# New ranks, gate counts and matmul estimates for the planner of a woven instruction order

## The chip, the core and the metric

The kernel runs on one core of one Trainium2 chip. A core has five engines that run side by side, each with its own fixed order of instructions: TensorE (PE in the profile; its weight loads stand apart as PEld), VectorE (DVE), ScalarE (ACT), GpSimd (POOL) and SyncE (SP), which issues most DMA transfers. Engines wait for each other by semaphores. The metric is the time of one execution on the device in microseconds, as the median of several runs.

## The reference

One layer of a diffusion backbone, batch 1, 256 latent tokens and 256 context tokens, width 2048, all in fp32. Cut to what matters:

```python
h  = modulate(rmsnorm(x, norm1_w), sh1, sc1)       # latent tokens
hc = modulate(rmsnorm(ctx, norm1_w), csh1, csc1)   # context tokens
cols = h @ w_in                                    # and hc @ w_in: one combined projection
# branch a, RWKV-7: 16 heads of 64, in both directions, context first
s = s * w_t - (s @ kk_t) * b_t + v_t * k_t ; y_t = s @ r_t
# branch b, gated DeltaNet: 8 heads of 128, chunks of 64, in both directions
sol = triangular_solve(lmat, rhs)                  # unit lower triangular, per chunk
s = s * gl_i + kt_i.T @ (u_i - w_i @ s)
# merge, output projection, SwiGLU with 5632 hidden columns
m = sigmoid(g_a) * (o_a @ p_a) + sigmoid(g_b) * (o_b @ p_b)
x = x + gt1 * (m @ w_out)
x = x + gt2 * swiglu(modulate(rmsnorm(x, norm2_w), sh2, sc2), w_gate_up, w_down)
return rmsnorm(x, final_norm_w)
```

## The kernel before

A large matmul of this kernel (a gemm below) splits each fp32 operand into a high and a low part in a faster format and adds three products: high by high, high by low, low by high. The weights are loaded as raw fp32 (tile `wraw`), ScalarE casts the high part (`whi`) and VectorE subtracts to get the low part (`wlo`). One gemm of the projection has 16 slices of the contraction, so 48 matmuls, with 512 columns (k and v, latent and context) or 256 (r, q and the gates, latent alone).

The kernel has a first part (modulation, norm, the low-rank columns), the woven part, and then merge, output projection and feed-forward, written straight. Only the woven part is planned. It holds 8 pairs of RWKV heads, then 8 DeltaNet heads, and 86 projection gemms. Each piece of the work is a Python generator that yields its next operation, a list of operations, or the name of something it waits for:

- per pair `p`: `prepare` (token shift, decays, keys), `grams` for each direction (products of 64x64 tiles), `inverse` (triangular inverses by 16x16 blocks, with a trip through DRAM scratch, then 32x32 tiles on PE in PSUM tile `pi`), `values`, `scan` (eight dependent steps with 64-row tiles in PSUM tile `s`);
- per DeltaNet head `h`: `features` (convolution, norm), `tokens` (transposes), `decays`, `head_grams`, `head_inverse`, `head_scan`; `begin` runs once before them;
- `lowrank` and 32 `lowrank_out` for the low-rank decays and rates that every pair needs;
- `products`, which runs the gemms one after the other, with `cast` for their weights (two gemms ahead at most) and `gate_out` to store a gate;
- `ada_rest` with its `row_tile`s, modulation rows on VectorE.

The planner `Weave` keeps a clock for each engine ("lane"). In each turn `Weave.run` takes the piece whose next operation can start earliest, and among those that could start at the same time the one with the lowest rank. It emits the operation and adds its estimated cost, and for PE a charge `turn` when the shape of tile changes. The order in which operations were emitted is the order in which each engine runs them on the chip; the estimates themselves have no part in the execution. `hop` is the assumed delay from one engine to another, `own` that on the same engine, `dma` that of a transfer. `products` has the highest rank number among the users of PE, so gemm matmuls go in wherever nothing else can start.

The costs stand in `Lane` (lines 126 to 137), the constants `LAT` and `GATES_A`, `GATES_B` at lines 28 to 30, the ranks in the calls of `weave.add`. All woven operations are recorded under line 145 in the profile, since one helper issues them; tiles tell them apart. Gemm matmuls write `mm`.

Forty of the 86 gemms are gates, which nothing in the weave waits for. `products` takes the first gemm of its list whose need is met, and the gates stand last in the list. `GATES_A[p]` gates may be taken once pair `p - 1` is prepared, `GATES_B[h]` once the Gram products of head `h` are done:

```python
todo += [("g", p, ("prepared", p - 1, 0) if p else None) for p in range(NPAIR) for _ in range(GATES_A[p])]
todo += [("g", h, ("gram", h)) for h in range(NGH) for _ in range(GATES_B[h])]
```

Head `h + 2` reuses buffers of head `h`: `tokens`, `decays` and `head_grams` of `h + 2` wait for the scan of `h`. Each inverse waits for the one before it.

Of the kernel before, what the change touches and what calls it, by code (L numbers as in the profile page):

```python
# [18 lines left out]
P = 128  # L19
D = 2048  # L20
KT = D // P
T = 256
# [2 lines left out]
NPAIR = 8  # L25
NGH = 8
DECAY = 0.6065306597126334
GATES_A, GATES_B = ((6, 3, 0, 2, 3, 3, 1, 3), (3, 0, 0, 0, 0, 2, 6, 8))

LAT = dict(dma=2.4, hop=0.3, own=0.1, grp=32, crank=-1, cg=4, turn=0.13)  # L30
LNEXP = "natural_log_exp_and_others"
SIGM = "sigmoid_and_others"
UNIT = 64 * 64 + 64
# [77 lines left out]
class Lane:  # L111
# [5 lines left out]
    def __getattr__(self, name):  # L117

        def op(out, *a, **k):
            if name == "preload_act_table_set":  # L120
                return Op(self, 1.3, lambda: self.engine.preload_act_table_set(out))
            if name == "dma_start":
                return Op(self, 0.6 if self.each > 0.002 else 0.06, lambda: self.engine.dma_start(out, *a))
            n = int(np.prod(out.shape[1:]))
            kind = "full"
            if name == "transpose" and len(a) == 2:
                cost = 0.109
            elif name == "matmul":
                rows, m = a[0].shape[0], out.shape[0]
                if a[0].dtype == F32R:  # L130
                    cost, kind = 0.0035 + 0.000448 * n, "split"
                elif rows <= 64 and m <= 64:
                    cost, kind = 0.026 if rows < 64 else max(0.06, 0.05 + 0.00015 * n), (rows, m)
                elif m <= 64:
                    cost, kind = 0.085 if m == 64 else 0.12, (rows, m)
                else:
                    cost = (0.0054 + 0.00167 * n) * (1.22 if rows == 96 else 1)
            else:
                psum = a and getattr(a[0], "tensor", None) is not None and "PSum" in type(a[0].tensor).__name__
                cost = (self.psum if psum else self.fixed) + self.each * n  # L140
# [4 lines left out]
            return Op(self, cost, lambda: getattr(self.engine, name)(out, *a, **k), kind)  # L145
        return op


class Loads:
# [121 lines left out]
def emit(ctx: ExitStack, tc, A, out, dbg=None):  # L271
# [4 lines left out]
    weave = Weave()  # L276
# [132 lines left out]
    with tc.tile_pool(name="p0", bufs=1) as p0, \  # L409
# [31 lines left out]
        ps = pst(pa, "pa")  # L441
# [276 lines left out]
    def lowrank():  # L718
# [17 lines left out]
        for p in range(NPAIR):  # L736
# [8 lines left out]
            for j in (0, 2, 1, 3):  # L745
                ps = yield psb
                yield e.matmul(ps, w[:96, 4 * (p % 2) + j], lin[:, j], start=True, stop=True)
                weave.add(2, lowrank_out(p, j, ps, out[j]))

    def prepare(p):  # L750

# [75 lines left out]
        yield v.scalar_tensor_tensor(kb, kb, p_("rk", p), r, ALU.mult, ALU.mult)  # L827
        weave.ready("keys", p)
        if p + 1 < NPAIR:
            weave.add(10 * p + 13, prepare(p + 1))  # L830

    def grams(p, d):
        o = pr[p]
# [3 lines left out]
        def m4(a, b, rows):  # L837
# [1 line left out]


        p1, p2 = yield pab, pab
        yield [e.matmul(ps[h if src is ic else half[1 - j], 64 * c:64 * c + 64], src[h, T + 64 * c:T + 64 * c + 64],
                             lc[h, c, j, :], start=True, stop=True)
                    for c in range(4) for ps, src in ((p1, ic), (p2, kt)) for j, h in enumerate(half)]
        yield v.tensor_mul(LT[:, d, 4:8, :], c3(p1[:, 0:T]), m4(0, 64, slice(0, P)))
        weave.release(pab)
        for j in range(2):
# [4 lines left out]
        yield [e.matmul(ps[h if src is ic else half[1 - j], P * c:P * c + P], src[h, 64 * c:64 * c + 64], la[h, c, j, :],  # L852
                             start=True, stop=True) for c in range(4) for ps, src in ((p1, ic), (p2, kt)) for j, h in enumerate(half)]
# [183 lines left out]
    def products():  # L1037
# [24 lines left out]
        while todo or nxt:  # L1062
            if nxt is None:
# [3 lines left out]
                    continue  # L1067
                if nxt[0] == "g":
                    nxt = "g", next(gate_next)
                weave.add(LAT['crank'], cast(source(*nxt), i))  # L1070
            what, p = nxt
            nxt = choose()
            if nxt is not None:
                if nxt[0] == "g":
                    nxt = "g", next(gate_next)
                weave.add(LAT['crank'], cast(source(*nxt), i + 1))
            ps = yield mmb
            n = 512 if what in "kvKV" else T
            for k in range(KT):
# [6 lines left out]
                    weave.ready("read", i, k // 8)  # L1086
            i += 1
            if what == "g":
                weave.add(150, gate_out(rs, p, ps))
            else:  # L1090
                (hd if what in "KVQ" else pr)[p][what + "ps"] = ps
                weave.ready(what + "gemm", p)
# [326 lines left out]
    def ada_rest():  # L1419
# [23 lines left out]
        for i in range(4 * KT):  # L1443
            if i > 2:
                yield "added", i - 3
            if i % 8 == 0 and i:
                yield "gscan", i // 8 - 1
            weave.add(500, row_tile(i))
            if i % KT == KT - 1:
                b = i // KT  # L1450
                yield "added", i
# [288 lines left out]
```

## Time and profile before

| what | us |
|---|---|
| median of 3 runs | 2293.3 |
| lowest, highest | 2292.33, 2308.79 |
| span of the profiled execution, first to last instruction | 2286.3 |
| median less that span | 7.0 |
| PE busy in the span | 2184.5 |
| DVE, ACT busy in the span | 1561.3, 1056.6 |

The profile gives the execution that it records by its span; the time of a run holds some microseconds more around it. A busy time is the union of the instructions of an engine. Matmuls overlap, and the end of each is modelled, so a busy PE can still be one whose matmuls do not follow each other as fast as they could: the distance between starts tells that. In a row of grouped instructions stand line, engine, operation, written and read tiles, shape, count, then busy time, mean ns of one, and the idle time just before with what ended it. PEclk is the granted clock of TensorE.

### The profile page before, as it was taken

To read this page: it belongs to the slowest core of one execution; us is meant where nothing else is said; L and a number is where in the kernel's file an instruction comes from. 1 tells how busy PE (TensorE), PEld (TensorE's weight loads), DVE (VectorE), ACT (ScalarE), POOL (GpSimd) and SP (SyncE) were. 2 spreads that over 40 slices of the span, in tenths; PEclk is the share of its full clock that TensorE was granted. 3 is DMA by queue.
4 is the path that set the end of the run, shared out by engine and by line. 5 is a ranking of instruction groups with operands and counts; after the bars stand their busy time and mean duration, and the time that the engine had idled before them with its cause. 6 is when DMAs were issued, how large, how long until landed. Compare 5 with 4: busy or idle time off the path is not lost. (4 is left out here: it accounts for less than half of the span.)

```text
span 2286.3 us, 54678 instructions
## 1 busy us (share of the span) xinstructions
PE 2184.5 (96%) x22904; PEld 1925.0 (84%) x22904; DVE 1561.3 (68%) x3225; ACT 1056.6 (46%) x1922; POOL 110.3 (5%) x185
## 2 busy tenths in 40 slices
PE   7998999999999999999999989899999999999998
PEld 4766577777777788888888889889999999999997
DVE  3446588888877586899997668774656656444444
ACT  3245554544555554444453445444444444444443
POOL 0000000000000010111110040000000000000000
PEclk9999999999999999999999989999999999999999
DMA  9955643443443254555566696864777776566665
GB/s 384 407 148 170 187 113 89 117 106 99 106 101 100 87 180 141 162 163 165 167 188 216 232 350 230 283 207 142 237 238 236 236 233 214 186 185 192 186 189 162
DMA packets 231926, 430.76 MB, mean 188 GB/s; under 512 B 114944, under 2 KB 129152, under 8 KB 227328
## 3 DMA queue, kind: packets, MB, share of 16 engines
q1 hardware_dynamic: 203744, 350.72, 49.5%
q0 software_dynamic: 14112, 51.39, 7.1%
q10 hardware_dynamic: 13824, 25.17, 3.3%
q8 instruction: 179, 2.93, 0.5%
q14 instruction: 67, 0.55, 0.1%
HBM read 401.44 MB, written 25.77 MB: 187 GB/s over the span
## 5 line engine op out<-in xcount | busy, mean ns | idle before, releaser
L361 DVE TENSOR_TENSOR wlo<-wraw,whi 128x1024 fp32r<-128x1024 f32 x328 | 393.4, 1199 | 336.5 <-ACT whi L360 332.9
L360 ACT CAST whi<-wraw 128x1024 fp32r<-128x1024 f32 x328 | 337.5, 1029 | 469.2 <-PE mm L371 434.4
L145 PE MATMUL mm<-hxh,wlo 128*128 128x256 f32 (+1 forms) x1376 | 466.3, 339 | 7.3 <-DVE wlo L145 6.9
L145 PE MATMUL mm<-hxh,whi 128*128 128x256 f32 (+1 forms) x1376 | 464.7, 338 | 6.0 <-ACT whi L145 5.8
L145 PE MATMUL mm<-hxl,whi 128*128 128x256 f32 (+1 forms) x1376 | 462.2, 336 | 0.0
L372 PE MATMUL mm<-hfh,wlo 128*128 128x256 f32 x1344 | 374.9, 279 | 0.3 <-DVE wlo L361 0.3
L370 PE MATMUL mm<-hfh,whi 128*128 128x256 f32 x1344 | 374.9, 279 | 0.0
L371 PE MATMUL mm<-hfl,whi 128*128 128x256 f32 x1344 | 374.7, 279 | 0.0
L145 PEld LDWEIGHTS mm<-hxh,wlo 128*128 128x128 f32 x1376 | 262.4, 191 | 35.5 <-DVE wlo L145 10.0
L145 PEld LDWEIGHTS mm<-hxh,whi 128*128 128x128 f32 x1376 | 262.6, 191 | 33.3 <-ACT whi L145 7.2
L145 PEld LDWEIGHTS mm<-hxl,whi 128*128 128x128 f32 x1376 | 262.3, 191 | 25.2 <-issue 5.7
L145 DVE TENSOR_TENSOR wlo<-wraw,whi 128x512 fp32r<-128x512 f32 x344 | 236.1, 689 | 59.3 <-ACT whi L145 58.0
L372 PEld LDWEIGHTS mm<-hfh,wlo 128*128 128x128 f32 x1344 | 252.7, 188 | 0.5 <-DVE wlo L361 0.5
L370 PEld LDWEIGHTS mm<-hfh,whi 128*128 128x128 f32 x1344 | 252.8, 188 | 0.0
L371 PEld LDWEIGHTS mm<-hfl,whi 128*128 128x128 f32 x1344 | 252.7, 188 | 0.0
L145 ACT CAST whi<-wraw 128x512 fp32r<-128x512 f32 x344 | 205.0, 618 | 94.2 <-PE mm L145 56.9
L145 DVE TENSOR_TENSOR arena<-arena 128x512 f32<-128x512 f32 (+12 forms) x538 | 132.9, 248 | 28.2 <-DMA arena<-scr 13.5
L370 PE MATMUL mm<-za,whi 128*128 128x256 f32 x512 | 142.9, 279 | 0.0
L372 PE MATMUL mm<-za,wlo 128*128 128x256 f32 x512 | 142.7, 279 | 0.0
L371 PE MATMUL mm<-za,whi 128*128 128x256 f32 x512 | 142.7, 279 | 0.0
L370 PEld LDWEIGHTS mm<-za,whi 128*128 128x128 f32 x512 | 96.3, 188 | 0.0
L371 PEld LDWEIGHTS mm<-za,whi 128*128 128x128 f32 x512 | 96.3, 188 | 0.0
(318 smaller groups left out, 3907.5 us busy)
## 6 DMA issues: line engine op xcount, KB each, us to landing
wraw<-w SPq DMA_DIRECT2D x172, 512.0 KB, 4.1
wraw<-wgu SPq DMA_DIRECT2D x168, 512.0 KB, 4.5
aw<-ada_rest POOLq DMA_DIRECT2D x96, 512.0 KB, 5.2
aw<-ada_first SPq DMA_DIRECT2D x32, 1024.0 KB, 11.6
wraw<-wdn SPq DMA_DIRECT2D x64, 448.0 KB, 3.6
wraw<-wout SPq DMA_DIRECT2D x32, 512.0 KB, 4.8
aw<-ada_gt ACTq DMA_DIRECT2D x64, 256.0 KB, 4.8
wraw<-wdn SPq DMA_DIRECT2D x32, 512.0 KB, 3.6
```

The source lines that it names most:

```text
L145: return Op(self, cost, lambda: getattr(self.engine, name)(out, *a, **k), kind)
L360: S.copy(hi[:, c, :M], raw[:, c, :M])
L361: V.tensor_sub(lo[:, c, :M], raw[:, c, :M], hi[:, c, :M].bitcast(F32))
L370: E.matmul(ps, hi, Xh[:, k, :n], start=first and i == 0, stop=False)
L371: E.matmul(ps, hi, Xl[:, k, :n], start=False, stop=False)
L372: E.matmul(ps, lo, Xh[:, k, :n], start=False, stop=last and i == len(wt) - 1)
```

## The change

Three things change, all in what the planner reads; no operation is added, removed or given other operands.

The ranks, so far plain numbers at each `weave.add` (10 times the pair, 100 plus 10 times the head, plus a small number), come from a table `RANK`. The gate counts are new; their sum stays 40. Of the estimates, `hop`, `own` and `turn` are new; a matmul of 32-row tiles, of 64x64 tiles and of 128x64 tiles has a new cost; and the Gram products of the pairs, whose consecutive calls use four different 64x64 corners of the array, are charged half by a new function `quad`.

```diff
-GATES_A, GATES_B = ((6, 3, 0, 2, 3, 3, 1, 3), (3, 0, 0, 0, 0, 2, 6, 8))
-
-LAT = dict(dma=2.4, hop=0.3, own=0.1, grp=32, crank=-1, cg=4, turn=0.13)
+GATES_A, GATES_B = (10, 5, 6, 0, 1, 4, 3, 0), (0, 3, 0, 0, 0, 0, 4, 4)
+
+RANK = dict(cast=-24, lowrank=-14, prepare=24, grams=24, inverse=-1, values=7, scan=-60, begin=101, head_scan=144, head_inverse=44, head_grams=193, decays=99, tokens=163, features=141, gate_out=71, lowrank_out=42, row_tile=435)
+LAT = dict(dma=2.4, hop=0.299, own=0.072, grp=32, cg=4, turn=0.179)
...
                 elif rows <= 64 and m <= 64:
-                    cost, kind = 0.026 if rows < 64 else max(0.06, 0.05 + 0.00015 * n), (rows, m)
+                    cost, kind = (0.01 + 0.00037 * n if rows < 64 else 0.01 + 0.00075 * n), (rows, m)
                 elif m <= 64:
-                    cost, kind = 0.085 if m == 64 else 0.12, (rows, m)
+                    cost, kind = 0.058 if m == 64 else 0.14, (rows, m)
...
+def quad(ops):
+    for o in ops:
+        o.cost *= 0.5
+    return ops
...
-                weave.add(2, lowrank_out(p, j, ps, out[j]))
+                weave.add(RANK['lowrank_out'], lowrank_out(p, j, ps, out[j]))
...
-            weave.add(10 * p + 13, prepare(p + 1))
+            weave.add(10 * p + 10 + RANK['prepare'], prepare(p + 1))
...
-        yield [e.matmul(ps[h if src is ic else half[1 - j], 64 * c:64 * c + 64], src[h, T + 64 * c:T + 64 * c + 64],
+        yield quad([e.matmul(ps[h if src is ic else half[1 - j], 64 * c:64 * c + 64], src[h, T + 64 * c:T + 64 * c + 64],
                              lc[h, c, j, :], start=True, stop=True)
-                    for c in range(4) for ps, src in ((p1, ic), (p2, kt)) for j, h in enumerate(half)]
+                    for c in range(4) for ps, src in ((p1, ic), (p2, kt)) for j, h in enumerate(half)])
...
-                weave.add(LAT['crank'], cast(source(*nxt), i))
+                weave.add(RANK['cast'], cast(source(*nxt), i))
...
-                weave.add(150, gate_out(rs, p, ps))
+                weave.add(RANK['gate_out'], gate_out(rs, p, ps))
...
-            weave.add(500, row_tile(i))
+            weave.add(RANK['row_tile'], row_tile(i))
...
-        weave.add(2, lowrank())
-        weave.add(3, prepare(0))
+        weave.add(RANK['lowrank'], lowrank())
+        weave.add(RANK['prepare'], prepare(0))
         for p in range(NPAIR):
             for d in range(2):
-                weave.add(10 * p + 2, grams(p, d))
-            weave.add(10 * p + 1, inverse(p))
-            weave.add(10 * p + 4, values(p))
-            weave.add(10 * p, scan(p))
-        weave.add(100, begin())
+                weave.add(10 * p + RANK['grams'], grams(p, d))
+            weave.add(10 * p + RANK['inverse'], inverse(p))
+            weave.add(10 * p + RANK['values'], values(p))
+            weave.add(10 * p + RANK['scan'], scan(p))
+        weave.add(RANK['begin'], begin())
         for h in range(NGH):
-            for i, piece in enumerate((head_scan, head_inverse, head_grams, decays, tokens, features)):
-                weave.add(100 + 10 * h + i, piece(h))
+            for piece in (head_scan, head_inverse, head_grams, decays, tokens, features):
+                weave.add(10 * h + RANK[piece.__name__], piece(h))
```

More of the change, by code (lines that the diff above doesn't have):

```diff
@@ L851, in grams @@
         p1, p2 = yield pab, pab
-        yield [e.matmul(ps[h if src is ic else half[1 - j], P * c:P * c + P], src[h, 64 * c:64 * c + 64], la[h, c, j, :],
-                             start=True, stop=True) for c in range(4) for ps, src in ((p1, ic), (p2, kt)) for j, h in enumerate(half)]
+        yield quad([e.matmul(ps[h if src is ic else half[1 - j], P * c:P * c + P], src[h, 64 * c:64 * c + 64], la[h, c, j, :],
+                             start=True, stop=True) for c in range(4) for ps, src in ((p1, ic), (p2, kt)) for j, h in enumerate(half)])
         pv = p1.rearrange("p (c t) -> p c t", t=P)
@@ L1075, in products @@
                     nxt = "g", next(gate_next)
-                weave.add(LAT['crank'], cast(source(*nxt), i + 1))
+                weave.add(RANK['cast'], cast(source(*nxt), i + 1))
             ps = yield mmb
```

## Prediction

> **What bounds the kernel now.** I read the page first: the busy shares and the two strips over the span.
>
> ```profile
> span 2286.3 us, 54678 instructions
> ...
> PE 2184.5 (96%) x22904; PEld 1925.0 (84%) x22904; DVE 1561.3 (68%) x3225; ACT 1056.6 (46%) x1922; POOL 110.3 (5%) x185
> ...
> PE   7998999999999999999999989899999999999998
> ...
> PEclk9999999999999999999999989999999999999999
> ```
>
> TensorE (PE) carries the whole span; no other engine comes near it on average. The diff can act only between the first and the last woven instruction, so I cut the span by stage with the view of windows: start of the weave, pairs, heads, last heads, and what lies before and behind.
>
> ```profile
> core 0: us, PE busy (x) PEld busy (x) DVE busy (x) ACT busy (x) POOL busy (x), PEclk, DMA share, GB/s
> 0.00:130.00 130.00, 113.58 (x1340) 81.19 (x1341) 54.33 (x147) 37.06 (x70) 0.41 (x5) 0.97 0.97 365
> 130.00:260.00 130.00, 111.20 (x892) 78.21 (x890) 72.72 (x163) 73.93 (x123) 3.01 (x7) 0.95 0.60 181
> 260.00:820.00 560.00, 546.54 (x7843) 421.30 (x7840) 444.62 (x1108) 282.64 (x702) 19.95 (x49) 1.00 0.40 106
> 820.00:1180.00 360.00, 350.84 (x3540) 297.09 (x3539) 316.21 (x807) 172.97 (x341) 40.35 (x61) 1.00 0.57 167
> 1180.00:1312.00 132.00, 122.16 (x1399) 115.36 (x1397) 97.72 (x249) 61.14 (x130) 10.62 (x19) 0.96 0.65 209
> 1312.00:2287.00 975.00, 940.20 (x7900) 931.87 (x7900) 575.69 (x753) 428.87 (x560) 35.98 (x46) 0.98 0.68 218
> ```
>
> The weave is 1182 us. PE is idle in its four stages for 18.8, 13.5, 9.2 and 9.8 us, together 51.3. In the first and the last the granted clock is 0.95 and 0.96, which is 130 x 0.05 = 6.5 and 132 x 0.04 = 5.3 us of lost clock. Everything else is PE at work. The number of matmuls stays as it is, so a new order can only win idle time, lost clock, and what PE loses when it changes from one shape of tile to another. DVE at 316 of 360 us is the second engine among the heads.
>
> What PE waits for, within the weave (waits of PE, 130 to 1312 us):
>
> ```profile
> PE mm L145 <- DVE wlo L145: 6.9, 10, 1.8
> PE pa L145 <- ACT arena L145: 6.2, 6, 2.1
> PE pi L145 <- DVE arena L145: 6.1, 7, 2.3
> PE mm L145 <- ACT whi L145: 5.8, 5, 1.9
> PE pi L145 <- issue: 4.0, 6, 1.3
> PE s L145 <- DVE Vn L145: 3.9, 5, 2.7
> ```
>
> There is no single late resource: the gemms wait for the two casts (12.7 us), the inverses (pi) for VectorE or the sequencer (10.1 us), the others for small pieces. These are places where PE's fixed order got to an instruction earlier than the other engines' orders did.
>
> **The change part by part: the estimates.** The planner lays out every engine's order by its own costs. The rows of PE over 3 us of a pair, and two groups of Gram products, tell how good these are. An fp32 matmul stands in the trace as two records, so x64 is 32 calls and x8 is 4.
>
> ```profile
> 599.81 0.28 PE L145 MATMUL mm<-hxl,whi 128*128 128x256 f32 x1
> ...
> 601.91 0.28 PE L145 MATMUL mm<-hxl,whi 128*128 128x256 f32 x1
> 602.03 0.28 PE L145 MATMUL mm<-hxh,wlo 128*128 128x256 f32 x1
> 602.24 0.45 PE L145 MATMUL s<-VX,LAl 128*64 128x64 f32 x8
> 602.62 0.38 PE L145 MATMUL mm<-hxh,whi 128*128 128x256 f32 x1
> 602.93 0.73 PE L145 MATMUL pi<-arena 32*32 32x16 f32 x64
> 603.59 0.45 PE L145 MATMUL s<-R,Tx 64*64 64x64 f32 x8
> 603.87 0.39 PE L145 MATMUL s<-VX,C 64*64 64x128 f32 x4
> ...
> 615.71 1.24 PE L145 MATMUL pa<-LAl,arena 64*64 64x128 f32 x32
> 616.88 0.38 PE L145 MATMUL mm<-hxh,wlo 128*128 128x256 f32 x1
> ```
>
> Starts count here, not durations. Gemm to gemm is 0.117 us (19 steps from 599.81 to 602.03). Going from a gemm to a small tile takes 0.21, so 0.09 more. The lone gemm at 602.62 holds PE for 0.31, so a return and a new entry cost 0.19 together. With that, a visit of 32 calls of 32x32 tiles takes 0.66 + 0.19 = 0.85 us. The old estimate is 32 x 0.026 + 2 x 0.13 = 1.09, the new one 32 x 0.0159 + 2 x 0.179 = 0.87: now right. A visit of four 128x64 calls takes 0.38 + 0.19 = 0.57; old 4 x 0.085 + 0.26 = 0.60, new 4 x 0.058 + 0.358 = 0.59: no difference. Sixteen Gram calls with 128 columns take 1.17 + 0.19 = 1.36; old 1.37, new (halved by quad) 16 x 0.053 + 0.358 = 1.21: now too short by 0.15. So the old estimates were fair already, and the repair is mostly at the inverses, which is where PE came early and waited.
>
> ```profile
> L145 PE MATMUL pi<-arena,Tx 32*32 32x16 f32 x1536 | 17.6, 182 | 9.3 <-DVE arena L145 5.0 <-issue 4.0
> L145 PE MATMUL pi<-arena 32*32 32x16 f32 x1024 | 10.9, 180 | 0.8 <-DVE arena L145 0.8
> ```
>
> These are 24 and 16 visits of 64 records, each planned 0.22 us too long, 8.8 us in all, and 10.1 us of idle stand before them. I take 8.8, less the sixteen Gram visits that are now planned short (16 x 0.15 = 2.4): a gain of 6.4. Bounds: all 10.1 gained, or nothing gained and 2.4 lost. Behind a wait that goes, the same VectorE chain is late next, so the gain is no more than the idle shown.
>
> **The ranks.** Among the pairs the sequence of what runs side by side (scan of one, inverse and values of the next, Gram products and preparation of the one after) stays, and only its distances widen; scans 0 to 3 now go ahead of the casts. Among the heads it turns: the inverse goes first, decays ahead of the scan, Gram products last. No instruction and no wait is added; the same DMA issues, weight loads and the scratch transfers of the inverses among them, stand in another order in SP's queue. The rank of lowrank_out goes from 2 to 42, so that pair 0 passes the low-rank outputs, for all of which the preparation of pair 1 waits:
>
> ```profile
> L145 ACT ACTIVATE lo<-s,PR 128x512 f32<-128x512 f32 x32 | 21.9, 687 | 26.5 <-PE s L145 21.4 <-DMA sgd__1342<-lo 4.5 <-PE pa L145 0.5
> ```
>
> At worst pair 1 comes 22 us later; four more gates at the start (below) are 22 us of PE to hide it, and without them it would be 22 us of idle. At best the 18.8 us of idle there go. Where a cast now waits behind a scan's ScalarE copy, a gemm is late by one copy; the cover is the pair of casts made ahead. For a price below and above nothing: the gemms' cast waits are 12.7 us, and could double or go.
>
> **The gate counts.** Forty gate gemms are PE's filler. Cumulated over the pairs they were released 6, 9, 9, 11, 14, 17, 18, 21 and are now 10, 15, 21, 21, 22, 26, 29, 29. Behind the Gram products of heads 5, 6 and 7 there were 2 + 6 + 8 = 16; now 0 + 4 + 4 = 8. A gate is 48 matmuls of 0.117 = 5.6 us of PE, two 512 KB loads on SP's queue, four casts each on ScalarE and VectorE, and one copy out.
>
> ```profile
> wraw<-w SPq DMA_DIRECT2D x172, 512.0 KB, 4.1
> ...
> L145 ACT CAST whi<-wraw 128x512 fp32r<-128x512 f32 x344 | 205.0, 618 | 94.2 <-PE mm L145 56.9 <-issue 18.1 <-DMA wraw<-w 13.2
> L145 DVE TENSOR_TENSOR wlo<-wraw,whi 128x512 fp32r<-128x512 f32 x344 | 236.1, 689 | 59.3 <-ACT whi L145 58.0
> ```
>
> Per gate that is 2.5 us of ScalarE and 2.8 of VectorE. Four more at the start cost 10 and 11 us of engines that are busy 74 and 73 of 130 us there, with DMA at 0.60: they fit, and can fill PE while low-rank outputs drain. The 8 gates taken from the heads free 22 us of VectorE where it is scarce. The moved PE time itself is neither won nor lost.
>
> **The sum.** Start, pairs and first heads have 41.5 us idle and 6.5 us of lost clock. With the estimates worth 6.4, and ranks and fillers worth half of what remains, (48 - 6.4)/2 = 20.8, that is 27; I take 24, since the last heads, with fewer fillers, should rather lose 3 or 4 than gain. Half is a choice: PE already fills 97% of the pairs and heads, and a rearranged order makes waits of its own. The profiled execution has a span of 2286.3 us, the median of the three runs is 2293.3, so 7.0 lie around the span. Forecast: 2262.3 in the span, **2269 us** at the median, 1.1% less. Its own range is 2250 to 2288.
>
> On the clock: the rows have 0.95 and 0.96 where the longest single wait on PE is 2.7 us. The Trainium skill, "TensorE: Matmul & The Clock Gate", Part 1, says that PE falls to half clock after an idle window of about 3.4 us. By it none of these waits would cost clock and the sum would lack 3 us, 2272; the trace disagrees, and I go with the trace. On the tiles: the 0.09 and 0.19 us above fit what the skill says in "TensorEngine Tiling (Array Packing)", Key Properties, that a change of tiling mode drains TensorE; this speaks against ranks that jump to a small tile as soon as it is ready.
>
> **Rivals.** First, **the last heads starve** (slower). From the last PT product of head 7 to the end of the weave:
>
> ```profile
> 1225.19 0.40 DVE L145 TENSOR_TENSOR PT<-pa,arena 128x256 f32<-128x256 f32 x1
> 1226.18 0.42 DVE L145 STREAM_TRANSPOSE T<-LT 64x256 f32<-64x256 f32 x1
> ...
> 1280.51 0.62 ACT L145 COPY TF<-Tx 64x512 f32<-64x512 f32 x1
> ...
> 1310.20 0.28 PE L145 MATMUL mm<-hxh,wlo 128*128 128x256 f32 x1
> ...
> L145 ACT COPY arena<-mm 128x256 f32<-128x256 f32 x9 | 3.3, 372 | 19.9 <-PE mm L145 11.1 <-issue 8.8
> ```
>
> The inverse of head 7 starts at once and takes 54 us, its scan and the end 30 more; nine gates (50 us of PE) lie beside it. With four, 28 us of that cover are gone. If the chain keeps its 85 us, PE idles for 28 and loses about 5 of clock: 2293 + 33 = 2326, or 2302 with the gains of the forecast elsewhere. For it: the inverse begins 1 us after its input, so nothing is ahead of it to remove. Against it: much of the 54 us is queueing between gemms and row tiles, and the inverse now ranks first. It decides from the point where the chain stays over 57 us.
>
> Second, **Gram products ranked last stretch the heads** (slower). Features of the next head now go ahead of them on VectorE:
>
> ```profile
> L145 DVE SCALAR_TENSOR_TENSOR arena<-mm,PR,arena 128x508 f32<-128x508 f32 (+3 forms) x96 | 62.2, 648 | 4.5 <-ACT arena L145 4.1
> ```
>
> Twelve per head are 7.8 us. Heads h and h+2 are chained by the scan that frees the buffers, so three rounds would lose 23 us, with hardly a gate there to fill it: 2316. It needs the next head's gemms to be done by then.
>
> Third, **fewer changes of tile as well**. The new planner charges 0.179 for each, so its order may make fewer. A visit costs 0.19; the timeline of PE has seven returns from small tiles to the gemm in the 25 us from 600 (the first is that at 602.62), some 160 for the 560 us of the pairs, and as many again for the start and heads by a like rate: 60 us in all. A third of it is 20: 2249.
>
> Fourth, **nothing to tell**: new waits take the place of the old, 2286 to 2293. It includes that the estimates, fair before, hardly change the plan.
>
> **How the numbers follow.** The forecast 0.42 (0.24 of it over 1% faster, 0.18 within), fewer changes 0.16, starving last heads 0.20 (0.13 over 1% slower, 0.07 within), stretched heads 0.14 (0.10 slower, 0.04 within), nothing 0.08. So 0.40 faster, 0.37 within 1%, 0.23 slower; 1% is about what these runs, 2292.3 to 2308.8, can tell from no change. The range, 2240 to 2330, takes in fewer changes at its low end and the starved end at its high end and leaves out about 0.08 on either side.
>
> **What would show it.** Right: PE idle between the weave's ends near 27 us, pi waits under 4 us, an unchanged 22904 PE records, a clock of 0.97 or more in the first stage. The weave then ends about 1286. Wrong: a PE stretch under 85% busy in the last 60 us of the weave with pi or s waiting (starved), distances between the heads' transposes T<-LT over 57 us (stretched), or the same 51 us of idle at other places. If the time falls by much more than the idle does, the changes of tile went, and the lone gemm matmuls between small groups should be rarer.

## The result: no difference, and the profile after

The changed kernel takes 2296.0 us at the median (2287.3 to 2309.1), the kernel before, run beside it, 2298.6 us (2287.8 to 2308.8). The ratio is 1.0002, with a 95% interval of 0.9989 to 1.0016. The gain of 1.1% that was forecast is not there.

The page of the kernel after: its span and the busy shares.

```profile
span 2289.3 us, 54680 instructions
...
PE 2192.2 (96%) x22904; PEld 1928.6 (84%) x22904; DVE 1558.0 (68%) x3225; ACT 1059.9 (46%) x1923; POOL 113.3 (5%) x185
```

The stages of the kernel after (columns: window, length, busy time of PE, PEld, DVE, ACT, POOL, then granted clock, DMA share, GB/s):

```profile
130.00:260.00 130.00, 111.51 (x681) 81.56 (x680) 75.75 (x166) 71.20 (x121) 2.42 (x7) 0.92 0.59 176
260.00:820.00 560.00, 544.69 (x8002) 414.17 (x8000) 433.06 (x1081) 283.36 (x696) 18.45 (x44) 0.98 0.39 103
820.00:1180.00 360.00, 352.78 (x3526) 296.48 (x3525) 316.06 (x816) 175.75 (x345) 44.00 (x63) 1.00 0.57 168
1180.00:1312.00 132.00, 126.03 (x1464) 120.00 (x1463) 101.64 (x262) 62.18 (x132) 11.24 (x19) 0.97 0.71 222
```

PE's idle time in the four stages is 18.5, 15.3, 7.2 and 6.0 us, 47.0 together: 4.3 less than before. But the granted clock is now 0.92 in the first stage and 0.98 among the pairs, where it was 0.95 and 1.00. Lost clock is the length of a stage times (1 - clock). From these clocks of two digits that is 130 x 0.08 + 560 x 0.02 + 132 x 0.03 = 25.6 us, against 11.8 before. These are one execution each, and the clock of a stage varies: the first stage has 0.91 to 0.96 in the traces of other kernels below that keep this order. The weave ends where it did: the last product of the last scan (`s<-arena,C`) starts at 1310.6 us, before at 1308.8, not 24 us earlier.

What PE waits for in the weave of the kernel after (waits of PE, 130 to 1312 us: total, times, longest):

```profile
PE pi L146 <- issue: 8.5, 8, 2.8
PE s L146 <- DMA wraw<-lora: 7.1, 2, 4.9
PE mm L146 <- DVE wlo L146: 6.9, 6, 3.6
PE mm L146 <- ACT whi L146: 5.4, 4, 2.0
PE pa L146 <- ACT arena L146: 4.2, 6, 0.9
```

The inverses' 6.1 us of waiting for VectorE are down to 0.4. In their place stand 8.5 us in which the inverses wait for nothing that the profile shows ("issue", 4.0 before), and 7.1 us for the load of low-rank weights. The two waits of the inverses together hardly changed: 10.1 us before, 8.9 after, where under 4 were forecast.

**The account used for every run below.** Two rows give a kernel's TensorE: busy time on its page, and the mean granted clock over the span. For the kernels before and after:

```profile
core 0: 2286.3 us, clock 0.985
```

```profile
core 0: 2289.3 us, clock 0.980
```

Idle is span less busy; lost clock is span times (1 - clock); what is left is work at full clock. Before: 101.8 + 34.3, work 2150.2. After: 97.1 + 45.8, work 2146.4. The work is the same within 4 us. Idle fell by 4.7, lost clock rose by 11.5. This is bookkeeping for one execution of each: it says where the time lies, not why. The clock holds over all runs: its mean is 0.984 to 0.985 in five sets of runs of the kernel before, 101 in all, and 0.980 in the 20 runs of the kernel after, which is some 8 to 10 us more of lost clock.

### The profile page after: what moved, and what is told of

The parts are those of the page before. It is cut to its first block, busy times and chain, and to the rows that moved or that the text cites. A ratio compares the mean times of both kernels' runs of the same rounds, so it can differ in the third digit from the quotient of the medians.

```text
span 2289.3 us, 54680 instructions
## 1 busy us (share of the span) xinstructions
PE 2192.2 (96%) x22904; PEld 1928.6 (84%) x22904; DVE 1558.0 (68%) x3225; ACT 1059.9 (46%) x1923; POOL 113.3 (5%) x185
## 4 chain that ended last, share of the span: by engine, by line
PE 52%; DVE 7%; issue 7%; DMA 4%; ACT 4%; POOL 1%; SPq 0%; DVEq 0%; ACTq 0%; POOLq 0%
PE mm L379 13%; PE mm L377 12%; PE mm L378 12%; PE mm L146 9%; DVE arena L146 3%; PE s L146 3%; PE pa L146 2%; DMA wr<-wgu 1%; DVE wlo L146 1%; DMA aw<-ada_rest 1%; PE pi L146 1%; DVE wlo L368 1%; ACT arena L146 1%; ACT whi L367 1%; DMA gts__1351<-arena 0%
## 5 line engine op out<-in xcount | busy, mean ns | idle before, releaser
L377 PE MATMUL mm<-za,whi 128*128 128x256 f32 x512 | 142.9, 279 | 0.0
```

The source lines that it names most:

```text
L377: E.matmul(ps, hi, Xh[:, k, :n], start=first and i == 0, stop=False)
```

## The experiments

The planner has a clock of its own, the time that its costs add up to while the order is being built. "Planned end" below is that clock at the last woven instruction of PE (the first three expectations take the last of any engine, up to 2.2 us later). It is no measurement, but it is what ranks and counts of such a kernel can be picked by. It stands at 1147.1 us for the kernel before and at 1117.6 for the one after: 29.5 us of paper gain. All ratios are against the kernel before, run alongside.

| order | planned end | ratio, 95% | idle | lost clock | work |
|---|---|---|---|---|---|
| before | 1147.1 | | 101.8 | 34.3 | 2150.2 |
| after: all three parts | 1117.6 | 1.0002 (0.9989 to 1.0016) | 97.1 | 45.8 | 2146.4 |
| estimates alone | 1154.7 | 1.0108 (1.0085 to 1.0132) | 111.5 | 50.8 | 2148.4 |
| ranks and gate counts | 1149.3 | 1.0009 (0.9994 to 1.0024) | 102.6 | 39.0 | 2150.6 |
| gate counts alone | 1165.2 | 1.0060 (1.0042 to 1.0078) | 116.2 | 50.8 | 2140.8 |
| estimates and ranks | 1151.7 | 1.0115 (1.0089 to 1.0141) | 114.5 | 58.1 | 2152.4 |
| matmul costs alone | 1145.5 | 1.0108 (1.0084 to 1.0131) | 112.6 | 50.8 | 2146.3 |
| `turn` alone | 1194.7 | 1.0119 (1.0090 to 1.0149) | 120.0 | 32.4 | 2161.2 |
| searched order a | 1136.4 | 1.0023 (1.0006 to 1.0039) | 101.4 | 48.2 | 2147.4 |
| searched order b | 1136.6 | 1.0059 (1.0036 to 1.0082) | 104.6 | 55.3 | 2143.9 |
| searched order c | 1139.3 | 0.9947 (0.9929 to 0.9965) | 101.1 | 32.0 | 2150.9 |
| before, 7 free gates | 1157.3 | 1.0097 (1.0078 to 1.0115) | 115.0 | 55.6 | 2147.9 |
| before, 5 free gates | 1157.0 | 1.0025 (1.0012 to 1.0039) | 103.5 | 39.0 | 2150.6 |

Idle, lost clock and work are those of one profiled execution each, in us. For the last two rows the kernels' own planner ends at 1157.3 and 1157.0, where their expectations below have 1155.3 and 1156.1; the plans are equal either way. Over all thirteen orders the work stays within 2141 to 2161 us, while idle plus lost clock runs from 133 to 173. The work differs by less than 1%; the rest of what an order changes is in these two.

### The parts one by one

The first three runs put back all but one or two of the parts.

```diff
 # estimates alone: RANK and GATES as before
 # ranks and gate counts: LAT, matmul costs and quad as before
 # gate counts alone: only this line changed
+GATES_A, GATES_B = (10, 5, 6, 0, 1, 4, 3, 0), (0, 3, 0, 0, 0, 0, 4, 4)
```

> The kernel before with the new estimates alone (hop, own, turn, the costs of small tiles, quad), old ranks and old gate counts. Theory A (TensorE's work sets the woven part, and any sensible order comes out alike within 0.3%): 2291 to 2305 us, ratio 0.997 to 1.003. Rival B (the planner's own clock is right about differences, and the parts of the change cancel on the chip): by that clock the weave ends at 1154.8 instead of 1148.2, so about 7 us or 0.3% slower; if on the other hand the estimates repair the waits at the inverses, as the prediction had it, 6 us faster and under 4 us of waits of pi.

> New ranks and new gate counts with the old estimates. Theory A: within 0.3% of before. Rival B: the planner's clock ends at 1151.5, 3 us later than before, so ratio 1.001, and if the ranks bring the low-rank outputs late by themselves, 5 to 10 us slower with a wait for the lora weights like that after the change (7.1 us).

> New gate counts alone, old ranks and estimates. Theory A: within 0.3%, and the times at which gates are copied out stay almost where they were, because a released gate is only taken when no other gemm is ready. Rival B: the planner's clock ends at 1167.4, 19 us later than before, ratio 1.008, with idle time of TensorE in the last heads, which have 8 gates less behind them.

Measured: 2313.5, 2291.4 and 2305.9 us, with 2291.7 for the kernel before. The estimates, forecast to win 6.4 us, lose 22 alone. Gate counts alone lose 14, gate counts with ranks nothing. The parts don't add up. Theory A holds for ranks with gate counts and fails for the other two. Rival B has about the right size for the gate counts (1.008 forecast, 1.0060 measured) and for ranks with gate counts, but the estimates cost 22 us where its plan has 7. With the estimates alone the heads have less filler: five gates are copied out between 820 and 1180 us, before it was nine. Their stage:

```profile
820.00:1180.00 360.00, 342.37 (x3387) 278.50 (x3383) 303.13 (x787) 169.39 (x335) 42.15 (x60) 0.97 0.50 146
```

PE is idle there for 17.6 us, against 9.2 before and 7.2 after.

Two more split the estimates, and one adds the ranks to them.

```diff
 # matmul costs alone: LAT, RANK, GATES as before, these and quad as after
+                    cost, kind = (0.01 + 0.00037 * n if rows < 64 else 0.01 + 0.00075 * n), (rows, m)
+                    cost, kind = 0.058 if m == 64 else 0.14, (rows, m)
 # turn alone: everything else as before
+LAT = dict(dma=2.4, hop=0.3, own=0.1, grp=32, cg=4, turn=0.179)
 # estimates and ranks: everything as after but
+GATES_A, GATES_B = ((6, 3, 0, 2, 3, 3, 1, 3), (3, 0, 0, 0, 0, 2, 6, 8))
```

> The kernel before with the new matmul costs and quad alone; hop, own and turn, ranks and gate counts as before. Theory C (TensorE's real work does not change with the planner's prices, so what counts is the idle time of TensorE in the plan, not the plan's end): the plan has 70.8 us of idle against 28.4 in that of the kernel before, 42 us more, so about 2334 us, ratio 1.018. Rival D (the plan's end is what counts): it ends at 1145.5 against 1147.1, so 2290, ratio 0.999.

> The kernel before with turn at 0.179 instead of 0.13 and nothing else. Theory C: the plan has 46.2 us of idle, 18 more than before, so about 2310 us, ratio 1.008. Rival D: the plan ends at 1194.7, 48 us later, so about 2340, ratio 1.021.

> New estimates and new ranks with the old gate counts. Planned end 1151.7 us, against 1154.7 with the estimates alone and 1117.6 with all three. Theory F (the three parts fit each other as picked, and only the whole is as good as before; one part put back is a random other order): 2300 to 2316 us, ratio 1.004 to 1.011. Theory K (the new ranks are what makes up for the estimates): 2290 us, ratio 1.000, the gate counts then do nothing. Gates put back are put back too in the start: with six instead of ten free of any need, pair 0's scan starts by 286 us (kernel after 293) under both.

2313.4 and 2315.4 us against 2291.0, and 2316.1 against 2293.1. So the new matmul costs lose as much by themselves as all the estimates do, and the ranks alone don't make it good: theory K falls. Theory F, that the values only fit as a set, has this run just past the upper end of its range, but it is too strong: ranks and gate counts come out level without the new estimates. Neither C (2334 and 2310 us) nor D (2290 and 2340) met the two split runs; C came within 6 us for `turn`. Neither the idle time in a plan nor its length ranks these orders: the matmul costs alone end 1.6 us earlier on paper and 22 later on the chip.

### Is a plan at least good under the old estimates?

A random search, under the estimates of the kernel before, kept ranks and gate counts that ended earliest on the planner's clock. Three such orders were run.

```diff
 # order a
+RANK = dict(cast=-17, lowrank=-9, prepare=48, grams=313, inverse=-84, values=85, scan=-48, ...)
+GATES_A, GATES_B = (7, 3, 0, 1, 2, 7, 0, 0), (1, 0, 5, 1, 0, 3, 1, 9)
 # order b
+GATES_A, GATES_B = (7, 5, 1, 0, 3, 2, 2, 2), (1, 0, 1, 0, 7, 6, 3, 0)
 # order c
+RANK = dict(cast=-79, lowrank=-279, prepare=114, grams=12, inverse=-30, values=-29, scan=15, begin=135, head_scan=55, head_inverse=105, head_grams=176, decays=48, tokens=136, features=217, gate_out=203, lowrank_out=-148, row_tile=271)
+GATES_A, GATES_B = (6, 3, 0, 5, 1, 2, 0, 1), (3, 8, 0, 0, 3, 5, 0, 3)
```

> The estimates of the kernel before, with ranks and gate counts picked by a random search that kept whatever ended earliest on the planner's own clock: first order, planned end 1136.4 us against 1147.1 for the kernel before (10.7 less), planned idle of PE 18.6 against 28.4. Theory P (the old estimates rank orders as the chip does, so a shorter plan is a shorter run): 2280 us, ratio 0.9953, PE idle in the profiled execution 92 or less against 101.8. Theory C (which order is picked by such small planned differences doesn't carry over; what the plan doesn't know, queues in order, sequencer stalls and the clock, gives it back): ratio 0.998 to 1.008, idle plus lost clock 136 to 150 us, as in the kernel before or more.

> As the order before it, second order of the same kind: planned end 1136.6 us (10.5 less than the kernel before), planned idle 19.2. Theory P: 2280 us, ratio 0.9954. Theory C: ratio 0.998 to 1.008, and the distance to the first order, for equal plans, up to 0.006.

> Third order of the same kind: planned end 1139.3 us (7.8 less than the kernel before), planned idle 21.4. Theory P: 2283 us, ratio 0.9966. Theory C: ratio 0.998 to 1.008, and the three need not stand in the order of their plans.

Planned gains of 10.7, 10.5 and 7.8 us came out as +0.2%, +0.6% and -0.5%. The two best plans of the three are the two slower kernels, so theory P falls: the old estimates don't rank such orders either. Theory C has a and b in its range. Order c fell below it, and lies close to what P gave for it (0.9966). Since one of three can look best by chance, c was run again.

> The third searched order once more, since one of three that comes out best can be best by chance: 0.993 to 0.997 if its gain of 0.5% is its own, 0.998 to 1.002 if it was the draw of the runs.

2281.3 us against 2294.5, ratio 0.9947 (0.9931 to 0.9964): **order c beats the kernel before** by half a per cent, and with it the one after, which is level with that. Its stages in the first run:

```profile
130.00:260.00 130.00, 112.59 (x830) 79.04 (x832) 73.33 (x164) 73.56 (x123) 3.62 (x7) 0.93 0.62 185
260.00:820.00 560.00, 546.13 (x7922) 421.01 (x7915) 443.05 (x1101) 283.49 (x698) 19.23 (x45) 0.99 0.39 102
820.00:1180.00 360.00, 351.76 (x3515) 294.25 (x3515) 316.61 (x815) 176.03 (x344) 42.96 (x64) 1.00 0.57 170
1180.00:1312.00 132.00, 122.47 (x1432) 115.93 (x1431) 102.15 (x257) 64.14 (x137) 11.47 (x20) 0.99 0.70 223
```

Its weave has hardly less idle than the kernel before (49.1 us in these windows against 51.3), and its clock is lower at the start and higher at the end. That isn't stable: the trace of its second run has 0.96 at the start and 0.97 at the end. Why just this order is the better one isn't shown.

### Where the first 11 us are lost

In the plan pair 0's scan stands some 5 us earlier after than before. On the chip it starts 11.4 us later, at 293.1 instead of 281.7 us. The timeline of PE shows what stands ahead of it. Before:

```profile
244.41 0.39 PE L145 MATMUL mm<-hxh,whi 128*128 128x512 f32 x1
245.32 8.67 PE L145 MATMUL s<-lin,wraw 96*128 96x512 f32 x16 [0.52 <-DMA wraw<-lora]
...
281.72 0.39 PE L145 MATMUL s<-R,Tx 64*64 64x64 f32 x6
```

and after:

```profile
250.29 0.40 PE L146 MATMUL mm<-hxl,whi 128*128 128x512 f32 x1
250.52 0.40 PE L146 MATMUL mm<-hxh,wlo 128*128 128x512 f32 x1
255.78 10.24 PE L146 MATMUL s<-lin,wraw 96*128 96x512 f32 x16 [4.87 <-DMA wraw<-lora]
265.95 1.38 PE L146 MATMUL pi<-arena 32*32 32x16 f32 x128
...
293.12 0.45 PE L146 MATMUL s<-R,Tx 64*64 64x64 f32 x8
```

In both, pair 0's inverse (`pi`) has its place in PE's order behind a block of low-rank products (`s<-lin,wraw`). Before, that block ends at 254.0. After, PE reaches it 6.1 us later, then waits 4.87 us for the block's weights, with all of its order queued behind; the block itself takes 1.6 us more, partly at half clock, and the inverse starts at 265.95. The load of these weights stands in SP's queue behind the inverse's own trips through scratch. Before, and then after:

```profile
241.33 0.33 SPq L156 DMA_DIRECT2D wraw<-lora  x1
```

```profile
247.72 0.70 SPq L163 DMA_DIRECT2D Tx<-tscr  x1
248.53 0.55 SPq L163 DMA_DIRECT2D wraw<-lora  x1
```

The kernel before issues the load ahead of them. The inverse's data is on its way at 247.7, two us earlier than before (249.72): it isn't the chain that is late but the place in the order. To take the queue out, the four low-rank loads were issued from GpSimd.

```diff
-                yield dq(w[:96], A["lora"][p // 2])
+                yield gq(w[:96], A["lora"][p // 2])
```

> The changed kernel with one difference: the four loads of the lora weights go out on GpSimd's DMA queue instead of SyncE's. If these loads stand behind the scratch transfers of pair 0's inverse in SyncE's queue, the 7.1 us of waits for them go and some of the half-clock stretches between 229 and 277 us with them: 5 to 12 us faster than the changed kernel, ratio 0.995 to 0.998. If the loads are late for another reason, or the stage is held by the ScalarE outputs, the wait passes to the next engine and the time stays within 3 us of the changed kernel.

Ratio 1.0004 (0.9991 to 1.0017). The wait for the load fell from 7.1 to 2.8 us, that for ScalarE's low-rank outputs rose from 2.1 to 5.7, and the inverse still started at 267.31. One wait passed into the next, so the place in the queue alone isn't the cause.

What the late starts have in common is the count of gates that are free at the start. With 5 or 6 the scan starts at 280 to 287 us in all seven kernels that were profiled with full work; with 7 or more at 293 to 297 in all seven. The ranks don't decide it: with the new ranks and six free gates it starts at 287.3 (by 286 was expected), with the old ranks and ten at 296.7. In the kernel after, the seventh gate leaves PE at 209 us and the eighth only at 286: more free gates than seven find other gemms ready. Two kernels, the one before with a single gate moved one way or the other, have equal plans:

```diff
-GATES_A, GATES_B = ((6, 3, 0, 2, 3, 3, 1, 3), (3, 0, 0, 0, 0, 2, 6, 8))
+GATES_A, GATES_B = ((7, 2, 0, 2, 3, 3, 1, 3), (3, 0, 0, 0, 0, 2, 6, 8))   # or (5, 4, 0, ...)
```

> The kernel before with one gate moved from the second pair to the first: 7 gates free of any need (7, 2, 0, 2, ...), and nothing else. Planned end 1155.3 us (8 more than the kernel before), pair 0's scan planned 1 us later. So far the kernels with six free gates start that scan at 280 to 287 us, those with seven or more at 289 to 298. Theory S (the seventh gate puts pair 0's inverse behind the third batch of low-rank outputs, and that is lost for good): the scan starts at 293 to 298, the end is 12 us behind the kernel with five free gates, about 2313 with 2293 for the kernel before. Theory N (the later scan is made up, since TensorE did a gate meanwhile): the scan starts as late, but the end is level with the kernel with five free gates within 4 us.

> The kernel before with one gate moved from the first pair to the second: 5 gates free of any need (5, 4, 0, 2, ...). Planned end 1156.1 us, as with seven. Both theories: pair 0's scan starts at 278 to 287, the end is 2298 to 2304 us. Theory S has it 12 us before the kernel with seven, theory N level with it.

2317.0 us with seven, 2299.9 with five, 2294.5 for the kernel before. With seven free gates, PE's timeline:

```profile
254.86 11.25 PE L146 MATMUL s<-lin,wraw 96*128 96x512 f32 x16 [6.19 <-DMA wraw<-lora]
266.04 1.39 PE L146 MATMUL pi<-arena 32*32 32x16 f32 x128
...
294.49 0.45 PE L146 MATMUL s<-R,Tx 64*64 64x64 f32 x8
```

and with five:

```profile
255.50 1.04 PE L146 MATMUL pi<-arena 32*32 32x16 f32 x60 [2.05 <-DMA arena<-tscr]
...
282.61 0.45 PE L146 MATMUL s<-R,Tx 64*64 64x64 f32 x8
```

The scan comes 12 us later with seven, as theory S said, and the end 17 us later where it said 12. In this pair theory N falls. That the lateness alone made the end late isn't shown, since the moved gate changes the rest of the order too, and it is no fixed price: ranks and gate counts under the old estimates have the late scan too (297 us) and end level with the kernel before.

Nor did the changed kernel stay behind. The first of the heads' transposes comes 16.8 us later than before, the last one only 2.3 us later (1226.18 before, in the prediction). Before, then after:

```profile
814.13 0.43 DVE L145 STREAM_TRANSPOSE T<-LT 64x256 f32<-64x256 f32 x1
830.89 0.43 DVE L146 STREAM_TRANSPOSE T<-LT 64x256 f32<-64x256 f32 x1
1228.51 0.91 DVE L146 STREAM_TRANSPOSE T<-LT 64x256 f32<-64x256 f32 x2
```

In these two executions the change lost 16.8 us up to the heads and won 14.5 back among them: "no difference" is the sum of the two. Of the 16.8, scan 0's 11.4 are followed above; the rest isn't.

### What holds the weave's length

If PE's work holds a stage, work that is taken out shortens it. Eight gates were left out but for one matmul each, in the last heads, the heads or the pairs; then two loads of VectorE.

```diff
 # 47 of 48 matmuls of eight gates, p from 32 (last heads), from 17 (heads) or from 8 (pairs)
+                    if what == "g" and 32 <= p < 40 and k + j:
+                        op.call = lambda: None
 # 120 modulation multiply-adds
+                    op.call = lambda: None
 # 26 of the 30 substitution steps in each head's inverse
+            if nu == 8 and 0 < j < 14:
+                o1.call = o2.call = lambda: None
```

> The changed kernel in its own order, with 47 of the 48 matmuls left out of each of the last 8 gate gemms (so these gates are wrong); loads, casts and copies stay. It takes 8 x 47 x 0.117 = 44 us of TensorE out of the last heads. If the last heads are held by TensorE's work: 40 to 44 us faster, ratio 0.981. If the inverse and scan of head 7 hold them (the rival of the starving last heads): 0 to 15 us faster and TensorE idle instead, with half clock.

> The same for the gate gemms 17 to 24, which lie one per head between 800 and 1160 us. If these heads are held by TensorE's work: 40 to 44 us faster, ratio 0.981. If the loop of scan, Gram products and inverse over two heads holds them: under 20 us faster, and idle time of TensorE in their place.

> The changed kernel in its own order, with 47 of 48 matmuls left out of each of the gate gemms 8 to 15, which lie one per pair between 310 and 715 us. It takes 44 us of TensorE out of the pairs. Theory F (a chain of dependent steps holds pairs and heads alike, and gates fill what it leaves): under 10 us faster. Rival (TensorE's work holds the pairs): 35 to 44 us faster.

> The changed kernel in its own order, with the 120 multiply-adds of the modulation rows left out on VectorE (so those rows are wrong): 120 x 0.77 = 92 us less of VectorE, nearly all beside the heads, and none of it in a chain that a head waits for. Theory F: under 12 us faster. Rival (VectorE's sheer load holds the heads, at 316 of 360 us): 50 us faster or more.

> The changed kernel in its own order, with 26 of the 30 small VectorE steps of the substitution left out in the inverse of each DeltaNet head (so the inverse is wrong): about 26 x 0.235 = 6 us out of the chain of each head and 49 us of VectorE in all. Theory F with the loop over two heads as the chain (scan, Gram products, inverse, scan): about four inverses of the eight lie on it behind one another, and the time falls by 24 us, at most 49 if all eight follow each other. Rival (it is not the inverse's chain that holds the heads): under 10 us faster, as with the modulation rows.

| left out of the kernel after | median, us | ratio, 95% | idle + lost clock | work |
|---|---|---|---|---|
| nothing | 2296.0 | 1.0002 (0.9989 to 1.0016) | 142.9 | 2146.4 |
| 8 gates in the last heads, 44 us of PE | 2289.2 | 0.9999 (0.9984 to 1.0015) | 191.0 | 2099.5 |
| 8 gates among the heads | 2296.4 | 1.0025 (1.0011 to 1.0040) | 188.5 | 2106.5 |
| 8 gates among the pairs | 2302.2 | 1.0044 (1.0021 to 1.0067) | 203.2 | 2098.1 |
| 120 modulation multiply-adds, 74 us of VectorE | 2288.7 | 0.9998 (0.9977 to 1.0019) | 142.8 | 2144.7 |
| substitution steps, 31 us of VectorE | 2287.8 | 0.9983 (0.9964 to 1.0001) | 118.5 | 2155.4 |

Not one of the three removals of PE work made the kernel faster, and the one among the pairs made it slower. The work falls by 40 to 48 us, as it must, and idle and lost clock rise by as much or more. The stages from which the gates were taken, last heads, heads and pairs in turn, each from its own kernel:

```profile
1180.00:1312.00 132.00, 94.79 (x1090) 83.67 (x1088) 101.08 (x261) 66.87 (x141) 12.17 (x20) 0.79 0.79 257
```

```profile
820.00:1180.00 360.00, 326.60 (x3152) 261.44 (x3151) 315.16 (x812) 175.93 (x349) 45.99 (x65) 0.94 0.56 167
```

```profile
260.00:820.00 560.00, 518.23 (x7530) 383.71 (x7530) 427.57 (x1069) 276.53 (x683) 16.38 (x42) 0.91 0.39 102
```

With these fillers gone PE's granted clock falls to 0.79, 0.94 and 0.91, from 0.97, 1.00 and 0.98. PE is busy for only 31, 26 and 26 us less there, not for 44, so what is left of its work takes longer. It stands idle for those 31, 26 and 26 us, so its work isn't all that these stages wait for; how much the lower clock of the matmuls that are left adds isn't told apart. Taking work off VectorE (267.89 us busy of 360 among the heads instead of 316.06) changed nothing. Leaving out the substitution, in the middle of the heads' chain, measured 0.2% with an interval that reaches no change; its theory F expected 24 us, its rival under 10. Its profiled execution was a good one (span 2273.9, clock 0.988); the median isn't. So neither the amount of PE's work nor VectorE's load nor this piece of the chain alone holds the weave. Which steps do stays open.

## Why the prediction was wrong, point by point

**What bounds the kernel: right as bookkeeping, wrong as a limit.** "A new order can only win idle time, lost clock, and what PE loses when it changes from one shape of tile to another" held in all thirteen orders: the work stayed. But "TensorE (PE) carries the whole span" doesn't hold for the weave: 40 to 48 us less of PE's work made it no shorter.

**The step that failed is the sum**: "ranks and fillers worth half of what remains, (48 - 6.4)/2 = 20.8". It took idle time and lost clock as a stock from which a new order draws. In fact each of the thirteen orders had about as much of them or more: 136 us before, 143 after, 133 to 173 over all. The runs with gates left out show why idle time isn't simply there to be won: with 40 to 48 us of PE's work taken out, idle time and lost clock grew by 46 to 60 and the time stayed, so more than the amount of PE's work holds the weave's length. What that is stays open. The text said that "a rearranged order makes waits of its own" and then priced these new waits at half of the old; measured, 47.0 us of idle stand where 51.3 stood, and more lost clock than before. A forecast of no change would have been right. The measured 2296 lies above the forecast's own range of 2250 to 2288, within the wide one of 2240 to 2330, which takes in gain and loss alike.

**The estimates, forecast +6.4 us, alone cost 22.** The reading of a 32x32 visit as 0.85 us stands, and the inverses' waits for VectorE fell, to 3.2 us with the estimates alone and to 0.4 with all three parts, though the "issue" waits rose in their place. What failed is the low bound, "nothing gained and 2.4 lost". A cost moves the whole order behind it, so what it can lose isn't bounded by the waits at its own instruction: the new matmul costs alone lost the whole 22 us. The list of costs was short, too. `quad` halves a second group of Gram products (`pa<-LAc`, 512 records), which was left out, and `turn` is charged at every change of shape: raising it alone put 48 us on the plan and 24 on the chip.

**The ranks.** The low-rank outputs were rightly singled out, but the wrong pair was costed: "at worst pair 1 comes 22 us later". It was pair 0 that came late, by 11.4, since PE's order still has a block of low-rank products ahead of pair 0's inverse. That goes with the gate counts, not with the ranks. The prediction named SP's queue and gave it no price; moving the late load to another queue won nothing.

**The gate counts.** "The moved PE time itself is neither won nor lost" was wrong: alone they cost 14 us. "They fit" was worked out from the load of ScalarE and VectorE; what moved with them is the order of PE, where pair 0's scan starts 12 us later with seven free gates than with five. Nor did the counts move as they read: in the last stage 15 gates end after and 14 before, since a released gate is taken only when no other gemm is ready.

**The median against the span.** "7.0 lie around the span" came from a median that belonged to other executions. The profiled execution after took 2291.13 us with a span of 2289.3: 1.8 lie around it.

**The clock.** It was right to hold with the trace that waits shorter than 3 us cost clock; the window at 417 us below shows it once more, with 0.92 as its longest. But only a gain was booked for it, 0.97 or more in the first stage, where 0.92 was measured.

**The rivals.** The last heads didn't starve: PE is busy for 126.0 of their 132 us. The heads weren't stretched: from the first to the last T<-LT transpose are 397.6 us after and 412.1 before, so they got shorter. The changes of tile didn't fall by a third: counted in the traces, the tile's shape changes 663 times among the woven matmuls before and 674 times after, and PE returns to the gemm 461 and 455 times, where the prediction had some 320. "Nothing to tell", with 0.08 the smallest chance of all, was right that new waits would take the place of the old. It was wrong that the plan would hardly change, since the plan became 29.5 us shorter.

## What to carry to other kernels

Ranks and counts picked on a planner's clock fit that clock: planned gains of 8 to 30 us came out between 12 us faster and 14 us slower here, and only the runs showed which. Before forecasting for such a change, take span, idle and lost clock apart and ask which of the things that the planner doesn't know (order in a DMA queue, waits without a shown cause, clock) the new order touches; without an answer the forecast is no change. Check by taking work out whether the busiest engine sets the time at all. And look at what stands ahead of the first link of a chain in every queue that the link passes, PE's own included.

## What was not expected of the hardware

**PE's clock fell with no long wait.** Windows of the kernel after around 420 us:

```profile
413.60:417.00 3.40, 3.40 (x41) 2.99 (x39) 3.31 (x9) 0.00 (x0) 0.00 (x0) 1.00 0.48 153
417.00:420.40 3.40, 2.48 (x146) 2.08 (x146) 2.23 (x4) 1.35 (x4) 0.00 (x0) 0.99 0.23 92
420.40:430.60 10.20, 10.20 (x187) 7.69 (x181) 8.05 (x19) 3.03 (x9) 0.00 (x0) 0.50 0.16 43
430.60:434.00 3.40, 3.40 (x80) 2.58 (x79) 1.30 (x4) 2.26 (x6) 0.00 (x0) 1.00 0.76 200
```

and the timeline of PE in the second of them:

```profile
417.22 0.73 PE L146 MATMUL pi<-arena 32*32 32x16 f32 x64
417.88 0.45 PE L146 MATMUL s<-R,Tx 64*64 64x64 f32 x8
418.25 0.45 PE L146 MATMUL s<-LAl,VX 128*64 128x64 f32 x8
418.64 0.66 PE L146 MATMUL pi<-arena 32*32 32x16 f32 x57
420.22 0.25 PE L146 MATMUL pi<-arena 32*32 32x16 f32 x7 [0.92 <-issue]
...
426.08 0.63 PE L146 MATMUL mm<-hxl,whi 128*128 128x512 f32 x1
426.51 0.63 PE L146 MATMUL mm<-hxh,wlo 128*128 128x512 f32 x1
```

The one wait in those 3.4 us is 0.92 us, and PE counts as busy for 2.48, but with small tiles alone. Then the clock is halved for 10.2 us: gemm matmuls of 512 columns stand 0.43 us apart instead of the 0.23 from 250.29 to 250.52. So gemms between small tiles seem not only to fill PE but to keep its clock up. It fits that the kernel with fewer gates among the pairs had a clock of 0.91 there and was slower, but that kernel's PE was also idle for more of the stage (41.8 us against 15.3), so small tiles and idle time aren't told apart. The Trainium skill, "TensorE: Matmul & The Clock Gate", Part 1, has PE fall to half clock after an idle window of about 3.4 us, with windows that run freely. The length of the stretch, three such windows, agrees; that the window must be idle doesn't agree with 2.48 of 3.40 us busy.

**PE waits within bursts of small matmuls, for nothing that the profile shows.** In the kernel after, 95 of 128 records of 32x32 products follow each other in 0.98 us, and then PE waits 2.83 us for nothing that the profile shows:

```profile
268.62 0.98 PE L146 MATMUL pi<-arena,Tx 32*32 32x16 f32 x95
272.43 0.45 PE L146 MATMUL pi<-arena,Tx 32*32 32x16 f32 x33 [2.83 <-issue]
```

The same visit has a wait of 3.38 us behind 94 records with the loads on GpSimd's queue, and of 2.91 behind 95 with seven free gates. In the kernel before it is 1.08 us behind 26 records; with five free gates the visit runs through. What causes it wasn't tried.
